# Gate and up projections of a float32 encoder layer with rows on partitions instead of hidden columns

## The chip, the core and the metric

The kernel runs on one core of a Trainium2 chip. A core has a matrix engine (TensorE, in the profile PE, with PEld for its weight loads), VectorE (DVE), ScalarE (ACT), GpSimd (POOL) and SyncE (SP); SP, ACT and POOL each issue DMAs from a queue of their own. Matmuls write to PSUM, eight banks of 128 partitions by 512 floats. Everything else lies in SBUF, 128 partitions wide, or outside in DRAM. The metric is the device time of one execution in microseconds (us), the median over runs.

## The reference

One encoder layer over 256 rows of 2048 features: a block of four mixers, a cross attention over 256 memory rows, and a SwiGLU feed-forward, each added to the residual, then a last normalisation. What the change touches is the last part:

```python
def swiglu(h, w_gate_up, w_down):
    gate, up = jnp.split(h @ w_gate_up, 2, axis=-1)
    return (jax.nn.silu(gate) * up) @ w_down
...
x = x + swiglu(rms_norm(x, norm_g[l, 2]), w_gate_up[l], w_down[l])
return rms_norm(x, final_norm_g)
```

`w_gate_up` is 2048 x 11264 (twice D_FF = 5632), `w_down` 5632 x 2048.

## The kernel before

Each float32 matrix product is made of reduced-precision (float32r) parts: an operand is split into a high part and the remainder (`split`, L202: ScalarE casts the high part, VectorE subtracts), and high x high, high x low and low x high are summed in PSUM. An activation tile, or slot, is 128 features by 512: 256 rows' high parts, then their low parts. Weights come as one stream, `Stream`: the host packs them in the order of use, 16 blocks of 128 x 128 to a 1 MB slab. SP loads slabs into three `raw` buffers. `_half` (L77) splits half a slab (8 blocks) into `wh` (cast on ScalarE, L104) and `wl` (subtraction on VectorE, L105), three buffers each. `take` (L109) hands out blocks, and makes halves so that two lie ahead of the one in use.

There are two ways to multiply. In `gemm`/`mm` (L294 to L341) a weight block is the stationary operand: one matmul of `wh` with all 512 columns of the slot (L301), one of `wl` with the 256 high ones (L302). The output has columns of the weight on partitions, and `merge` (L308) adds the two parts. In `gemm_rows` (L343) and in `prod` within `down` the slot is stationary and four weight blocks stream by: three matmuls of 512 columns for each half of the rows (L353 to L355, L785 to L787). The output has rows on partitions.

Work beside the matmuls is put in order by `Background`: generators that yield a delay. After each matmul step `poll` (L154) goes through those that are due, by the matmul time that has passed (`pe`) and the VectorE time still owed (`dve`, less than `OWED` = 0.9). `drain` runs one to its end. The instructions so traced get their final place on each engine from a scheduler; `keep_place` (L219) ties an instruction behind the one traced before it on its engine.

`mlp` (L724) runs after the attention, whose last product `w_xo` goes through `gemm`. Its input is `h3`, 16 slots, of which the last four are split by `rest` (L571) while the first matmuls run. Over 44 pairs of column tiles (gate, up) `gemm` makes 16 matmul pairs each; the first four tiles run over k = 0 to 11, then over 12 to 15. The evacuation `ev` merges, multiplies by the row factor `rs` (from `rstd_later`: sums of squares by L247, a factor for each row, spread over a bank by L278), takes the Silu on ScalarE (L735), multiplies by up, and splits the product into `f[j]`, the slot that down needs. So the 44 slots of `f` stand ready, features on partitions, with no turning.

`turn` (L751) brings the first 12 of 16 residual tiles to rows on partitions meanwhile: VectorE transposes 32 x 32 blocks within a tile (L758), four DMAs write the blocks to their places in `xrows` outside (L761), and six DMAs read rows back (L765). POOL issues these.

`down` (L772) multiplies `f` by `w_down`, with rows on partitions, in four quarters `c` of 512 output columns, k = 0 to 43 in each. After quarters 0 to 2 the residual is added and squares are summed. Quarter 3 begins by turning the residual's last four tiles on PE into its PSUM banks (eight matmuls, L818), so that the products are added to them. Its last 12 k are held back and run one half of the rows after the other, with the normalisation behind each. The last 32 blocks of the weights lie in `st.places`, here the slots of `h3`, free by then.

Of the kernel before, what the change touches and what calls it, by code (L numbers as in the profile page):

```python
# [13 lines left out]
F32 = mybir.dt.float32  # L14
# [21 lines left out]

HELD = 32

ROWS = ((256, 512), (768, 832), (NBLK - 16 * FT, NBLK))

LATE = 12

# [125 lines left out]
class Block:  # L168
# [171 lines left out]
        if last:  # L340
            group(n - 4, 4, last, before_last)  # L341

    def gemm_rows(self, w, col, slots, done=None):  # L343

        nc = self.nc
        ps = [self.gbank() for _ in range(2)]
        nk = len(slots)
        for k in range(nk):
            wh, wl = self.st.take(w, k, col, 4)
            for r in range(2):  # L350
                hi = slots[k][:, r * P:(r + 1) * P]
                lo = slots[k][:, R + r * P:R + (r + 1) * P]
                nc.tensor.matmul(ps[r][:, :], hi, wh, start=k == 0, stop=False)  # L353
                nc.tensor.matmul(ps[r][:, :], hi, wl, start=False, stop=False)  # L354
                nc.tensor.matmul(ps[r][:, :], lo, wh, start=False, stop=k == nk - 1)  # L355
            if done:
                done(k)
            self.bg.pe(1.407)
            self.bg.poll()
        return ps  # L360


    def run(self):
        nc, cp = self.nc, self.cp
        st = self.st
        self.act = [cp.tile([P, 512], F32R, name=f"act{i}") for i in range(24)]
        self.res = [cp.tile([P, 4, R], F32, name=f"res{i}") for i in range(4)]
        self.resk = lambda i: self.res[i // 4][:, i % 4, :]
        self.vec = cp.tile([P, NV], F32, name="vec")
        self.ones = cp.tile([P, P], F32, name="ones")  # L370
        self.ident = cp.tile([P, P], F32, name="ident")
        self.acc = cp.tile([P, R], F32, name="acc")
        self.mg = cp.tile([P, 16], F32, name="mg")
        self.eps = cp.tile([P, 8], F32, name="eps")[:, 0:1]
        self.gap(cp, 224)

        self.kd = nc.dram_tensor("keys", (P, 16 * R), F32, kind="Internal").ap()
        self.xr = nc.dram_tensor("xrows", (R, D), F32, kind="Internal").ap()
        self.vd = nc.dram_tensor("values", (P, 8 * 512), F32, kind="Internal").ap()
# [26 lines left out]
    def mixers(self):  # L406
# [76 lines left out]
        with tc.tile_pool(name="mid", bufs=1) as mid:  # L483
            gl = Gla(self, mid)
            with tc.tile_pool(name="hyp", bufs=1) as hyp, tc.tile_pool(name="k2", bufs=8) as k2:
                hy = Hyena(self, hyp, k2)

                mem0 = hy.piece()[:, 0:R + 16]
                nc.sync.dma_start(mem0, self.t["mem0"])
                self.bg.add(prepare(mid))  # L490

                def ev_k(i, p):
                    if i == 8:
                        for k in range(0, KT, 4):
                            self.load_x(k, 4)
                    nc.gpsimd.dma_start(self.kd[:, i * R:(i + 1) * R], self.merge(p))

                self.gemm("w_xkv", [i * P for i in range(16)], h, ev_k, first=(8, [[k] for k in range(KT)]), before=start_m)
                for hd in range(4):
                    for r, p in enumerate(self.gemm_rows("w_xkv", D + hd * 512, h, start_x if hd == 3 else None)):  # L500
# [12 lines left out]
                self.gemm("w_in", [256, 384, 0, 128], h, lambda i, p: gl.feed(i, self.merge(p)))  # L513
                for r, p in enumerate(self.gemm_rows("w_in", 512, h)):
# [209 lines left out]
    def mlp(self):  # L724
        tc, nc, act = self.tc, self.nc, self.act
        with tc.tile_pool(name="fp", bufs=1) as fp:
            self.gap(fp, 192)
            f = act[4:12] + [fp.tile([P, 512], F32R, name=f"f{i}") for i in range(36)]
            box = {}

            def ev(i, p):
                u = self.merge(p)
                self.tt(u, u, box["rs"], ALU.mult)
                if i % 2 == 0:
                    nc.scalar.activation(u, u, AF.Silu)  # L735
                    box["g"] = u
                else:
                    self.tt(u, u, box["g"], ALU.mult)
                    self.split(f[i // 2], u)

            cols = []
            for j in range(FT):
                cols += [j * P, DFF + j * P]
            ready = [self.late, self.bg.add(self.rstd_later(self.acc, D, box))]
            turned = self.bg.add(self.turn())
            self.gemm("w_gate_up", cols, self.h3, ev, first=(4, [list(range(12)), list(range(12, 16))]),
                      before=lambda n: n and [self.bg.drain(g) for g in ready])
            self.bg.drain(turned)
            self.down(f)

    def turn(self):  # L751

# [19 lines left out]
    def down(self, f):  # L772
# [2 lines left out]


        nc, st = self.nc, self.st
        h3 = self.h3
        st.places = [(h3[2 * i], h3[2 * i + 1]) for i in range(8)]
        ss = self.rp.tile([P, 24], F32, name="rc", tag="rc")  # L780

        def prod(p, r, k, wh, wl, start, stop):
            hi = f[k][:, r * P:(r + 1) * P]
            lo = f[k][:, R + r * P:R + (r + 1) * P]
            nc.tensor.matmul(p[:, :], hi, wh, start=start, stop=False)  # L785
            nc.tensor.matmul(p[:, :], hi, wl, start=False, stop=False)  # L786
            nc.tensor.matmul(p[:, :], lo, wh, start=False, stop=stop)  # L787
# [4 lines left out]
        def norm(p, r):  # L792
# [9 lines left out]
            for c in range(4):  # L802
# [6 lines left out]
                    nc.vector.tensor_scalar(out=x, in0=x, scalar1=a, scalar2=None, op0=ALU.mult)  # L809
                (nc.scalar if c == 1 else nc.sync).dma_start(self.t["out"][r * P:(r + 1) * P, c * 512:(c + 1) * 512], x)  # L810

        held = []
        for c in range(4):
            ps = [self.gbank() for _ in range(2)]
            if c == 3:
                for r in range(2):
                    for j in range(4):
                        nc.tensor.matmul(ps[r][:, j * P:(j + 1) * P], self.resk(12 + j)[:, r * P:(r + 1) * P], self.ident,  # L818
                                         is_transpose=True, start=j == 0, stop=False)
            for k in range(FT):  # L820
                wh, wl = st.take("w_down", k, c * 512, 4)
                if c == 3 and k >= FT - LATE:
                    held.append((k, wh, wl))
                    continue
                for r in range(2):
                    prod(ps[r], r, k, wh, wl, c < 3 and k == 0, c < 3 and k == FT - 1)
            if c < 3:
                for r in range(2):
                    x = self.half(c, r)
# [12 lines left out]
        nc.scalar.mul(fg[:, 3 * 512:4 * 512], fg[:, 3 * 512:4 * 512], 0.375)  # L842
        for r in range(2):
            for k, wh, wl in held:
                prod(ps[r], r, k, wh, wl, False, k == FT - 1)
            norm(ps[r], r)


# [540 lines left out]
```

## Time and profile before

| | us |
|---|---|
| median of 3 runs | 1506.02 |
| lowest, highest | 1505.64, 1507.26 |
| profiled execution | 1506.59 |
| its span, first to last instruction | 1504.8 |
| attention's last product ends, gate and up begin | about 762 |
| first matmul of down (L785) | 1250.4 |
| first turning matmul of the last quarter (L818) | 1435.2 |
| granted TensorE clock, mean | 0.999 of full speed |

How to read the profile: rows of the timeline give start, duration, engine, line, operation, out<-in and count, and in brackets the idle time before and what ended it. Rows of groups give line, engine, operation, out<-in, shape and count, then busy us and mean ns of one, then idle us before and what ended that. Matmuls are pipelined, and the duration of one overlaps the next, so their pace is the distance between starts. A row of waits or "idle before" counts only where the engine that waits is the one that others wait for.

### The profile page before, as it was taken

Reading aid. Unit: us, or ns where it says so; the run is one execution under the profiler, and the core shown is the slowest. Engines: PE = TensorE matmul, PEld = TensorE weight load, DVE = VectorE, ACT = ScalarE, POOL = GpSimd, SP = SyncE. Lnnn points to the kernel's source line nnn. Section 1 sums busy time; section 2 is a strip of 40 time slices with the busy share of each in tenths; the row PEclk is TensorE's granted clock in tenths of the full one; section 3 lists DMA queues with packets and bytes.
Section 4 is the critical chain, followed back from the end, with each engine's and each line's share of the span. In section 5 each row is a group of like instructions: output and inputs, shape, how many; then the busy total and the mean of one; then the engine's idle time right before and its main releaser. Section 6 shows DMA issues by size and latency. Waiting matters only on the chain.

```text
span 1504.8 us, 21369 instructions
## 1 busy us (share of the span) xinstructions
PE 1494.2 (99%) x8288; PEld 1288.5 (86%) x8288; DVE 997.8 (66%) x1551; ACT 784.7 (52%) x1236; POOL 68.6 (5%) x128
## 2 busy tenths in 40 slices
PE   9999999999999999999999999999999999999997
PEld 8887788889899888888888888888888888888886
DVE  6676768778776777877767666666666665444444
ACT  6565555547545556756555444444444444434344
POOL 0100100000000001100015100000000000000000
PEclk9999999999999999999999999999999999999999
DMA  9965554454446555544557655555555555555554
GB/s 355 347 245 202 187 197 160 151 193 143 177 155 216 193 196 203 191 149 170 194 179 248 211 181 190 195 196 182 185 193 196 191 182 186 196 188 179 193 193 142
DMA packets 51255, 294.68 MB, mean 196 GB/s; under 512 B 7086, under 2 KB 8399, under 8 KB 19537
## 3 DMA queue, kind: packets, MB, share of 16 engines
q1 hardware_dynamic: 45632, 281.11, 52.7%
q0 software_dynamic: 5088, 11.54, 2.3%
q8 instruction: 65, 1.06, 0.3%
q10 hardware_dynamic: 432, 0.66, 0.1%
q14 instruction: 38, 0.30, 0.1%
HBM read 285.42 MB, written 7.86 MB: 195 GB/s over the span
## 4 chain that ended last, share of the span: by engine, by line
PE 97%; ACT 1%; DVE 1%; DMA 0%; issue 0%; SPq 0%; ACTq 0%
PE pg L301 42%; PE pg L302 22%; PE pg L785 5%; PE pg L787 5%; PE pg L786 5%; PE pg L353 3%; PE pg L355 2%; PE pg L354 2%; PE pg L298 1%; PE pg L299 1%; PE pm L301 1%; PE pm L717 1%; PE pm L690 0%; PE pm L302 0%; DMA raw<-in_W 0%
## 5 line engine op out<-in xcount | busy, mean ns | idle before, releaser
L301 PE MATMUL pg<-act,wh 128*128 128x512 f32 x2704 | 945.9, 393 | 0.3 <-ACT wh L104 0.3
L105 DVE TENSOR_TENSOR wl<-raw,wh 128x1024 fp32r<-128x1024 f32 (+1 forms) x503 | 612.2, 1218 | 426.4 <-ACT wh L104 421.7
L104 ACT CAST wh<-raw 128x1024 fp32r<-128x1024 f32 (+1 forms) x503 | 524.7, 1044 | 589.0 <-PE pg L301 231.3
L302 PE MATMUL pg<-act,wl 128*128 128x256 f32 x2880 | 805.9, 280 | 0.2 <-DVE wl L105 0.2
L301 PEld LDWEIGHTS pg<-act,wh 128*128 128x128 f32 x2704 | 507.9, 188 | 112.7 <-ACT wh L104 0.6
L302 PEld LDWEIGHTS pg<-act,wl 128*128 128x128 f32 x2880 | 540.9, 188 | 2.3 <-issue 1.2
L785 PE MATMUL pg<-wh,f 128*128 128x512 f32 x272 | 107.9, 397 | 0.0
L787 PE MATMUL pg<-wh,f 128*128 128x512 f32 x272 | 107.8, 396 | 0.0
L786 PE MATMUL pg<-wl,f 128*128 128x512 f32 x272 | 107.6, 395 | 0.0
L196 DVE TENSOR_TENSOR tmp<-pg,tmp 128x256 f32<-128x256 f32 x174 | 72.6, 418 | 7.4 <-ACT tmp L308 6.1
L308 ACT COPY tmp<-pg 128x256 f32<-128x256 f32 x173 | 62.8, 364 | 11.4 <-PE pg L302 10.9
L353 PE MATMUL pg<-wh,act 128*128 128x512 f32 x160 | 64.0, 400 | 0.0
L355 PE MATMUL pg<-wh,act 128*128 128x512 f32 x160 | 63.0, 394 | 0.0
L354 PE MATMUL pg<-wl,act 128*128 128x512 f32 x160 | 62.9, 393 | 0.0
L787 PEld LDWEIGHTS pg<-wh,f 128*128 128x128 f32 x272 | 51.3, 189 | 12.0
L786 PEld LDWEIGHTS pg<-wl,f 128*128 128x128 f32 x272 | 51.3, 189 | 11.9
L785 PEld LDWEIGHTS pg<-wh,f 128*128 128x128 f32 x272 | 51.4, 189 | 11.8
L298 PE MATMUL pg<-act,wh 128*128 128x256 f32 x176 | 50.6, 288 | 0.0
L299 PE MATMUL pg<-act,wh 128*128 128x256 f32 x176 | 49.3, 280 | 0.0
L196 DVE TENSOR_TENSOR tmp<-tmp,rs 128x256 f32<-128x256 f32 x88 | 37.1, 423 | 2.7
L353 PEld LDWEIGHTS pg<-wh,act 128*128 128x128 f32 x160 | 30.1, 188 | 9.5 <-issue 1.7
L355 PEld LDWEIGHTS pg<-wh,act 128*128 128x128 f32 x160 | 30.1, 188 | 6.5
(263 smaller groups left out, 1222.8 us busy)
## 6 DMA issues: line engine op xcount, KB each, us to landing
raw<-in_W SPq DMA_DIRECT2D x246, 1024.0 KB, 4.8
raw<-in_W SPq DMA_DIRECT2D x11, 512.0 KB, 7.5
res<-in_xT SPq DMA_DIRECT2D x8, 512.0 KB, 5.8
k<-in_mem SPq DMA_DIRECT2D x8, 256.0 KB, 7.9
k<-in_x SPq DMA_DIRECT2D x8, 256.0 KB, 9.0
keys<-tmp POOLq DMA_DIRECT2D x16, 128.0 KB, 5.7
values<-tmp POOLq DMA_DIRECT2D x16, 128.0 KB, 2.1
mr<-keys POOLq DMA_DIRECT2D x16, 128.0 KB, 5.0
```

The source lines that it names most:

```text
L104: nc.scalar.copy(wh[:, a:b], r[:, a:b])
L105: nc.vector.tensor_tensor(out=wl[:, a:b], in0=r[:, a:b], in1=wh[:, a:b].bitcast(F32), op=ALU.subtract)
L196: self.nc.vector.tensor_tensor(out=out, in0=a, in1=b, op=op)
L298: self.nc.tensor.matmul(p[:, 0:R], wh, slot[:, 0:R], start=start, stop=False)
L301: self.nc.tensor.matmul(p[:, :], wh, slot[:, :], start=start, stop=False)
L302: self.nc.tensor.matmul(p[:, 0:R], wl, slot[:, 0:R], start=False, stop=stop)
L353: nc.tensor.matmul(ps[r][:, :], hi, wh, start=k == 0, stop=False)
L354: nc.tensor.matmul(ps[r][:, :], hi, wl, start=False, stop=False)
L355: nc.tensor.matmul(ps[r][:, :], lo, wh, start=False, stop=k == nk - 1)
L785: nc.tensor.matmul(p[:, :], hi, wh, start=start, stop=False)
L786: nc.tensor.matmul(p[:, :], hi, wl, start=False, stop=False)
L787: nc.tensor.matmul(p[:, :], lo, wh, start=False, stop=stop)
```

## The change

Gate and up now go through `gemm_rows`, which takes one or more column groups at once and works in parts. Eleven times a group of 512 gate columns and one of 512 up columns are made, rows on partitions (the first time both together, k = 0 to 11 and 12 to 15). The row factor is then one number per partition, an operand of the Silu and of the product. The product is turned back by VectorE's 32 x 32 transposes and eight DMAs to a DRAM tensor `hidden`; four DMAs read slots' worth of it back, and `fetch` splits them into `f`. The first 28 slots are fetched during gate and up, three reads ahead; the last 16 take the tiles of `h3` and are fetched during down, six ahead. The last weights' places become 16 tiles of their own. The turning of the residual's last quarter moves ahead of down's first quarter, into two `pm` banks that are kept. `ROWS`, which sets an offset of the weight buffers for rows-on-partitions stages, now covers gate and up.

```diff
-ROWS = ((256, 512), (768, 832), (NBLK - 16 * FT, NBLK))
+ROWS = ((256, 512), (768, 832), (NBLK - 48 * FT, NBLK))
...
+    def part_rows(self, p, r, slot, wh, wl, start, stop):
+
+        hi, lo = slot[:, r * P:(r + 1) * P], slot[:, R + r * P:R + (r + 1) * P]
+        self.nc.tensor.matmul(p[:, :], hi, wh, start=start, stop=False)
+        self.nc.tensor.matmul(p[:, :], hi, wl, start=False, stop=False)
+        self.nc.tensor.matmul(p[:, :], lo, wh, start=False, stop=stop)
+        self.bg.pe(0.687)
+
+    def gemm_rows(self, w, cols, slots, done=None, parts=None, before=None):
+
+
+        ps = [[self.gbank() for _ in range(2)] for _ in cols]
         nk = len(slots)
...
+        for part, ks in enumerate(parts or [range(nk)]):
+            if before:
+                before(part)
+            for k in ks:
+                for p, col in zip(ps, cols):
+                    wh, wl = self.st.take(w, k, col, 4)
+                    for r in range(2):
+                        self.part_rows(p[r], r, slots[k], wh, wl, k == 0, k == nk - 1)
+                if done:
+                    done(k)
+                self.bg.poll()
         return ps
...
+            f = act[4:12] + [fp.tile([P, 512], F32R, name=f"f{i}") for i in range(20)] + self.h3
+            with tc.tile_pool(name="gp", bufs=2) as gp:
+                self.gate_up(gp, f)
+            with tc.tile_pool(name="hp", bufs=1) as hp:
+                self.gap(hp, 64)
+                held = [hp.tile([P, 512], F32R, name=f"held{i}") for i in range(HELD // 2)]
+                self.st.places = list(zip(held[0::2], held[1::2]))
+                self.down(f)
+
+    def gate_up(self, gp, f):
+
+        nc = self.nc
+        box, g, stored = {}, {}, []
+
+        def norm():
+            box["col"] = self.rstd_begin([[self.acc]], D)
+            yield
+
+        def gate(ps):
+            for r in range(2):
+                g[r] = gp.tile([P, 512], F32, name=f"g{r}", tag=f"g{r}")
+                nc.scalar.activation(g[r], ps[r], AF.Silu, scale=box["col"][:, r:r + 1])
+
+        def up(j, ps):
+            for r in range(2):
+                h, u = (gp.tile([P, 512], F32, name=n, tag=n) for n in ("h", "u"))
+                self.stt(h, ps[r], box["col"][:, r:r + 1], g[r], ALU.mult, ALU.mult)
+                self.bg.dve(512)
+                nc.vector.transpose(u, h)
+                to = self.ff[j * 512:(j + 1) * 512, r * P:(r + 1) * P].rearrange("(b f) t -> f b t", f=32)
+                for a in range(4):
+                    nc.gpsimd.dma_start(to[:, :, 32 * a:32 * a + 32],
+                                        u[32 * a:32 * a + 32, :].rearrange("f (b t) -> f b t", t=32))
+            stored.append(j)
+
+        def fetch(k0, k1, ahead, pause):
+
+            m = {}
+            for k in range(k0, k1 + ahead):
+                if k < k1:
+                    while len(stored) <= k // 4:
+                        yield
+                    m[k] = self.tmp()
+                    nc.gpsimd.dma_start(m[k], self.ff[k * P:(k + 1) * P, :])
+                if k >= k0 + ahead:
+                    mark = len(nc.cur_bb.bb.instructions)
+                    self.split(f[k - ahead], m.pop(k - ahead))
+                    self.keep_place(mark)
+                    self.have = k - ahead + 1
+                    yield pause
+
+        ready = [self.late, self.bg.add(norm())]
+        turned = self.bg.add(self.turn())
+        ps = self.gemm_rows("w_gate_up", [0, DFF], self.h3, parts=[range(12), range(12, 16)],
+                            before=lambda n: n and [self.bg.drain(g) for g in ready])
+        gate(ps[0])
+        up(0, ps[1])
+        early = self.bg.add(fetch(0, FT - 16, 3, 2.0))
+        for j in range(1, DFF // 512):
+            gate(self.gemm_rows("w_gate_up", [j * 512], self.h3)[0])
+            up(j, self.gemm_rows("w_gate_up", [DFF + j * 512], self.h3)[0])
+        for x in (turned, early):
+            self.bg.drain(x)
+        self.bg.add(fetch(FT - 16, FT, 6, SOON))
...
+        end = [self.bank() for _ in range(2)]
+        for r in range(2):
+            for j in range(4):
+                nc.tensor.matmul(end[r][:, j * P:(j + 1) * P], self.resk(12 + j)[:, r * P:(r + 1) * P], self.ident,
+                                 is_transpose=True, start=j == 0, stop=False)
         held = []
         for c in range(4):
-            ps = [self.gbank() for _ in range(2)]
-            if c == 3:
...
+            ps = end if c == 3 else [self.gbank() for _ in range(2)]
             for k in range(FT):
...
                 for r in range(2):
-                    prod(ps[r], r, k, wh, wl, c < 3 and k == 0, c < 3 and k == FT - 1)
+                    self.part_rows(ps[r], r, f[k], wh, wl, c < 3 and k == 0, c < 3 and k == FT - 1)
+                self.bg.poll()
+                while self.have < min(FT, k + 3):
+                    self.bg.step(self.bg.q[0])
```

More of the change, by code (lines that the diff above doesn't have):

```diff
@@ L341, in gemm @@
             group(n - 4, 4, last, before_last)
-    def gemm_rows(self, w, col, slots, done=None):
-        nc = self.nc
-        ps = [self.gbank() for _ in range(2)]
-        nk = len(slots)
[L348 to L359, printed above, removed]
+    def part_rows(self, p, r, slot, wh, wl, start, stop):
[6 more added lines that the diff above has]
+        ps = [[self.gbank() for _ in range(2)] for _ in cols]
+        nk = len(slots)
+        for part, ks in enumerate(parts or [range(nk)]):
[9 more added lines that the diff above has]
+                self.bg.poll()
         return ps
@@ L378, in run @@
         self.xr = nc.dram_tensor("xrows", (R, D), F32, kind="Internal").ap()
+        self.ff = nc.dram_tensor("hidden", (DFF, R), F32, kind="Internal").ap()
         self.vd = nc.dram_tensor("values", (P, 8 * 512), F32, kind="Internal").ap()
@@ L499, in mixers @@
                 for hd in range(4):
-                    for r, p in enumerate(self.gemm_rows("w_xkv", D + hd * 512, h, start_x if hd == 3 else None)):
+                    for r, p in enumerate(self.gemm_rows("w_xkv", [D + hd * 512], h, start_x if hd == 3 else None)[0]):
                         for c in range(2):
@@ L513, in mixers @@
                 self.gemm("w_in", [256, 384, 0, 128], h, lambda i, p: gl.feed(i, self.merge(p)))
-                for r, p in enumerate(self.gemm_rows("w_in", 512, h)):
+                for r, p in enumerate(self.gemm_rows("w_in", [512], h)[0]):
                     nc.scalar.copy(gl.v[r], p)
@@ L727, in mlp @@
             self.gap(fp, 192)
[L728 to L749, printed above, removed]
+            f = act[4:12] + [fp.tile([P, 512], F32R, name=f"f{i}") for i in range(20)] + self.h3
@@ L777, in down @@
         nc, st = self.nc, self.st
-        h3 = self.h3
-        st.places = [(h3[2 * i], h3[2 * i + 1]) for i in range(8)]
         ss = self.rp.tile([P, 24], F32, name="rc", tag="rc")
[L782 to L787, printed above, removed]
         def squares(x, c, r):
@@ L810, in norm @@
                 (nc.scalar if c == 1 else nc.sync).dma_start(self.t["out"][r * P:(r + 1) * P, c * 512:(c + 1) * 512], x)
+        end = [self.bank() for _ in range(2)]
[3 more added lines that the diff above has]
+                                 is_transpose=True, start=j == 0, stop=False)
         held = []
         for c in range(4):
-            ps = [self.gbank() for _ in range(2)]
-            if c == 3:
[L816 to L819, printed above, removed]
+            ps = end if c == 3 else [self.gbank() for _ in range(2)]
             for k in range(FT):
@@ L844, in down @@
             for k, wh, wl in held:
-                prod(ps[r], r, k, wh, wl, False, k == FT - 1)
+                self.part_rows(ps[r], r, f[k], wh, wl, False, k == FT - 1)
             norm(ps[r], r)
```

## The prediction

> **What bounds the kernel now.** I read the page's engine table first, then the chain of waits, then TensorE's timeline.
>
> ```profile
> span 1504.8 us, 21369 instructions
> PE 1494.2 (99%) x8288; PEld 1288.5 (86%) x8288; DVE 997.8 (66%) x1551; ACT 784.7 (52%) x1236; POOL 68.6 (5%) x128
> PE 97%; ACT 1%; DVE 1%; DMA 0%; issue 0%; SPq 0%; ACTq 0%
> ```
>
> PE works for 99% of the span and makes up 97% of the chain that ended last. VectorE and ScalarE have a third and a half of their time free. So an edit is worth what it changes in PE's own pace, plus any wait it gives PE. The pace is read as start to start in the timeline, since each record of 0.28 to 0.40 us overlaps the next. First and last row of three stretches, gate and up, then down's first quarter, then its last:
>
> ```profile
> 899.79 0.28 PE L302 MATMUL pg<-act,wl 128*128 128x256 f32 x1
> ...
> 933.76 0.28 PE L302 MATMUL pg<-act,wl 128*128 128x256 f32 x1
> ...
> 1259.72 0.40 PE L786 MATMUL pg<-wl,act 128*128 128x512 f32 x1
> ...
> 1299.85 0.40 PE L787 MATMUL pg<-wh,f 128*128 128x512 f32 x1
> ...
> 1439.73 0.39 PE L786 MATMUL pg<-wl,act 128*128 128x512 f32 x1
> ...
> 1479.78 0.39 PE L787 MATMUL pg<-wh,f 128*128 128x512 f32 x1
> ```
>
> The first holds 98 pairs of L301 and L302: 33.97 us / 98 = 0.3466 us a pair. The second holds 172 steps in 40.13 us: 0.2333 us a matmul. The third holds 175 steps in 40.05 us: 0.2289 us. **One loop, with one shape, runs at two paces**, 1.9% apart. Between the second and third lie only the eight turning matmuls L818. I looked for the same switch elsewhere:
>
> ```profile
> 302.45 0.28 PE L302 MATMUL pg<-act,wl 128*128 128x256 f32 x1
> 302.57 0.40 PE L353 MATMUL pg<-wh,act 128*128 128x512 f32 x1
> ...
> 303.97 0.40 PE L353 MATMUL pg<-wh,act 128*128 128x512 f32 x1
> ...
> 100.12 0.40 PE L355 MATMUL pg<-wh,act 128*128 128x512 f32 x1
> ...
> 101.52 0.39 PE L355 MATMUL pg<-wh,act 128*128 128x512 f32 x1
> 101.75 0.39 PE L988 MATMUL pm<-w3h,hs 128*128 128x512 f32 x1
> ...
> 106.92 0.39 PE L353 MATMUL pg<-wh,act 128*128 128x512 f32 x1
> ...
> 111.27 0.39 PE L354 MATMUL pg<-wl,act 128*128 128x512 f32 x1
> ```
>
> Rows-on-partitions matmuls that follow the L301/L302 pairs directly are slow: 302.57 to 303.97 is 6 steps of 0.233, and 100.12 to 101.52 is too. After other matmuls have come between (L988 at 101.75), they are fast: 106.92 to 111.27 is 19 steps of 0.229. So the pace is not a property of tile or shape. It is kept from how the run of matmuls began.
>
> **The change part by part.**
>
> *Matmuls of gate and up.* Before: 88 column tiles x 16 = 1408 pairs, 1408 x 0.3466 = 488.0 us. After: 22 column groups of 512 (gate and up, 11 each) x 16 x 6 = 2112 matmuls of 512 columns; the columns streamed are the same. At the fast pace 2112 x 0.2289 = 483.4 us, **-4.6 us**; at the slow one 492.7 us, **+4.7 us**. Which holds depends on whether something breaks the run. The new stage starts behind `w_xo`'s pairs, so slow. Then `norm` issues `rstd_begin`, the only other matmuls of the stage:
>
> ```profile
> 767.09 0.34 PE pm L247 x4
> 772.88 0.66 PE pm L278 x2
> 1435.35 0.87 PE pg L818 x8
> ```
>
> These are rows of the chain. L247 now lies 5 us into the stage and stays, between the second and the latest the twelfth k of the first round, as the part boundary drains it. I take it as a breaker like L988 and L818; some 24 matmuls before it at the slow pace cost 24 x 0.0044 = 0.1 us. L278, which spread the row factor over a bank, falls away, since the factor is now one number per partition: **-0.7 us**.
>
> The Trainium skill ("TensorE: Matmul & The Clock Gate", Back-to-back issue gap) gives an isolated warm matmul N/2.4 + 2.5 ns, whatever ran before it. By it four blocks cost 1300 ns before and 1295 ns after, in all -1.8 us, and down would not change. The measured 1386 and 1373 ns lie over 5% above, and the two paces contradict it.
>
> *Down.* The eight L818 matmuls (0.87 us) move from ahead of the last quarter to ahead of the first, cost unchanged, 0. They need `res` rows 12 to 15, done before gate and up begin, and two `pm` banks, which nothing else needs then but the squares; two remain. They sit ahead of all of down, so its first three quarters, 3 x 44 x 6 = 792 matmuls, go at 0.2289 instead of 0.2333: **-3.5 us**. If they don't set the pace, 0.
>
> *Evacuation.* Nearest rows:
>
> ```profile
> L105 DVE TENSOR_TENSOR wl<-raw,wh 128x1024 fp32r<-128x1024 f32 x498 | 609.5, 1225 | 423.4 <-ACT wh L104 418.7 <-PE pg L302 2.1 <-ACT tmp L308 1.2
> L104 ACT CAST wh<-raw 128x1024 fp32r<-128x1024 f32 x498 | 522.3, 1049 | 586.0 <-PE pg L301 231.3 <-issue 153.5 <-PE pg L787 133.3
> L991 ACT ACTIVATE k<-k,vec 128x512 f32<-128x512 f32 x8 | 5.8, 724 | 0.1
> L196 DVE TENSOR_TENSOR k<-k,pm 128x512 f32<-128x512 f32 x10 | 6.8, 685 | 6.3 <-PE pm L989 6.3
> L196 DVE TENSOR_TENSOR f<-tmp,f 128x256 fp32r<-128x256 f32 x36 | 15.1, 419 | 0.0
> L204 ACT CAST f<-tmp 128x256 fp32r<-128x256 f32 x36 | 14.6, 404 | 0.0
> L200 DVE SCALAR_TENSOR_TENSOR act<-res,vec,act 128x256 fp32r<-128x256 f32 x32 | 15.1, 479 | 0.0
> L758 DVE STREAM_TRANSPOSE tmp<-res 128x256 f32<-128x256 f32 x12 | 5.2, 435 | 0.0
> ```
>
> 512 columns cost 685/419 = 1.63 times 256. Per group of 512 hidden columns ScalarE has two Silus (0.72) and four casts (0.40), 3.1 us; VectorE two products (1.63 x 0.479 = 0.78), two transposes (0.71) and four subtractions (0.42), 4.7 us. Before, VectorE had six operations of 0.42 for each of four tiles, 10 us. All lies beside 44 us of matmuls: 0. PE needs the banks again only after 16 x 6 x 0.229 = 22 us; in the first round gate's banks finish three to six matmuls ahead of up's, which covers most of their Silus. Price if not covered: two Silus, 1.4 us, once.
>
> *The way outside.* Each group issues eight writes of 64 KB and four reads of 128 KB on POOL's queue.
>
> ```profile
> L761 POOL DMA_DIRECT2D xrows<-tmp x48: 582/582/609, 765.0 to 834.0; - x48
> ...
> DMA to landing us min/median/max: 1.8/3.7/6.7
> ...
> q1 hardware_dynamic: 1979, 14.38, 53.5%
> q0 software_dynamic: 1856, 2.62, 12.5%
> res<-xrows POOLq DMA_DIRECT2D x6, 256.0 KB, 5.4
> ```
>
> The old `turn` has the same 128-byte runs. The two queue rows are the window 764 to 842 us that it fills: 12.5% for 2.62 MB against 53.5% for 14.38, so 1.28 times the time per byte. The new 88 x 64 KB out and 44 x 128 KB back, 11.5 MB, take 11.5/2.62 x 12.5% x 78 us = 43 us of all 16 engines over 484 us: 9% on top of 53%. Weights (SP's queue) stay ahead. On POOL, behind the writes stand reads and `turn`'s issues; down needs `turn` only after its first quarter.
>
> The danger is the hand-over. Let E be the end of up's last matmul. Products and transposes finish at E+1.5 and E+3.0; the eighth write leaves POOL at E + 1.5 + 8 x 0.58 = E+6.2 and lands at E+9.9; the read waits for all eight, then 0.6 + 5.4: E+15.9. In code order the planner lets the first split pass once 2.8 us of evacuation are worked off (E+5.5), and each further one 2.75 us later. Group 0's first split stands at E+5.5, that of groups 1 to 6 at E+13.8; the last sixteen begin at E+5.5 too, with older data, behind eight writes: E+12. ScalarE would block 10.4, 2.1 (six times) and 6.5 us, and behind it stand the weight casts L104, for which VectorE and PE wait. The cover is two halves of weights ahead, 5.5 us, less 1.05 + 1.23 to make the next: 3.2 us. So code order gives 7.2 + 0 + 3.3 = 10.5 us. The other end is 0:
>
> ```profile
> 762.24 0.36 ACT L308 COPY tmp<-pg 128x256 f32<-128x256 f32 x1
> 764.06 1.05 ACT L104 CAST wh<-raw 128x1024 fp32r<-128x1024 f32 x1 [1.47 <-PE pg L301]
> 765.02 0.41 ACT L234 ACTIVATE tmp<-res 128x256 f32<-128x256 f32 x1
> ```
>
> L234 squares the residual L308 evacuated, and comes in the code before the cast of a later half; on ScalarE the cast runs first. Instructions that are not ready are set behind ready ones, so I expect the casts ahead of splits that wait. I take 0.8 us, near that end.
>
> **Sum.** -4.6 + 0.1 - 0.7 + 0 - 3.5 + 0.8 = -7.9 us. The profiled execution took 1506.59 us (span 1504.8, 1.8 around it), 0.6 above the median of 1506.02, so the median becomes 1498.1; I say **1498**.
>
> **Rivals.**
>
> *Hand-over blocks (slower).* Casts stay behind splits, and writes and reads land 2 us later than the medians (6.7 is on record): 9.2 + 6 x 0.9 + 5.3 = 20 us, giving 1506 - 8.7 + 20 = 1517. It decides from 8.7 us of stalls on, about what the medians in code order make, so it starts as a draw. For: eleven hand-overs, one queue. Against: the order above.
>
> *L247 doesn't break the run.* Gate and up slow, down fast: +4.7 - 0.7 - 3.5 + 0.8 = +1.3, 1507.3. For: L247 has one column, unlike L988 and L818; no row shows it ahead of such matmuls.
>
> *No breaker works.* The change doesn't do what it seems to: +4.7 - 0.7 + 0.8 = +4.8, 1510.8. Against: two switches, L818 itself one.
>
> *The paces mix.* Each short wait of PE sets the run anew, either way. At the mean of 0.2311 gate and up cost 2112 x 0.2311 = 488.1, no gain, and down 1.7 less: -0.7 - 1.7 + 0.8 = -1.6, 1504.4. Against: neither pace was left within 40 us above. (The skill's formula would land there too, at 1504.2.)
>
> **Chances.** Forecast 0.66 (own range 1495 to 1503, small hand-over stalls included), hand-over 0.15, L247 0.10, no breaker 0.05, mixed paces 0.04. 0.2% is 3 us, about what a measurement of this kernel can tell. Below 1503: 0.68, with a little of the rivals; above 1509: 0.19; between: 0.13. The low end is the sum without stalls (1497.3) less 0.9 if the turns fill a bubble and 1.3 for spread and records: 1495. The high end takes in the L247 case and half a hand-over: 1509.
>
> **What would show it.** Steps of 0.229 in gate and up after L247, and in all of down; 0.233 in either refutes that term. L818 directly behind the last up matmul. ScalarE and VectorE without waits for the read of the hidden rows; PE idle, or casts waiting behind such a split, would show the hand-over. Turned out wrong: a span above 1502.

## The result and the profile after

The changed kernel took **1498.24 us** (median of 6 runs, 1497.69 to 1499.18), the kernel before in the same series 1506.49 (6 runs, 1505.64 to 1507.26): ratio 0.9946, 95% interval 0.9933 to 0.9959. The profiled execution took 1498.32 us with a span of 1496.5. The page, its engine table and the shares of the chain:

```profile
span 1496.5 us, 19811 instructions
PE 1485.9 (99%) x7582; PEld 1254.2 (84%) x7582; DVE 938.3 (63%) x1373; ACT 759.3 (51%) x1125; POOL 149.7 (10%) x260
PE 97%; ACT 1%; DVE 1%; DMA 0%; issue 0%; SPq 0%; ACTq 0%
```

TensorE still sets the end, with some 700 matmuls fewer, and POOL's busy time has more than doubled by the way outside. Where the 8.3 us of span came from is read from three starts on TensorE: gate and up's first matmul, down's first matmul, the end. First two rows of the timeline of the kernel before, then two of the kernel after:

```profile
761.15 0.39 PE L301 MATMUL pg<-act,wh 128*128 128x512 f32 x1
...
1250.38 0.40 PE L785 MATMUL pg<-wh,act 128*128 128x512 f32 x1
```

```profile
761.23 0.39 PE L346 MATMUL pg<-wh,act 128*128 128x512 f32 x1
...
1246.01 0.60 PE L857 MATMUL pm<-ident,res 128*128 128x128 f32 x4
1246.36 0.48 PE L346 MATMUL pg<-wh,act 128*128 128x512 f32 x1
```

Gate and up went from 1250.38 - 761.15 = 489.2 us to 1246.36 - 761.23 = 485.1 us: 4.1 less, although they now hold the eight turning matmuls. From there to the end it is 1504.8 - 1250.4 = 254.4 before and 1496.5 - 1246.4 = 250.1 after: 4.3 less, 0.9 of it the turning that left. The paces, from the first and last row of a stretch in gate and up and one in down's first quarter, kernel after:

```profile
899.69 0.39 PE L348 MATMUL pg<-wh,act 128*128 128x512 f32 x1
...
939.97 0.39 PE L347 MATMUL pg<-wl,act 128*128 128x512 f32 x1
...
1259.74 0.39 PE L347 MATMUL pg<-wl,f 128*128 128x512 f32 x1
...
1299.79 0.39 PE L348 MATMUL pg<-wh,act 128*128 128x512 f32 x1
```

Each of the two has the step of 0.2289 us (40.28 us / 176, 40.05 us / 175). Both terms on which the forecast rested are there. The other matmuls of gate and up, rows of the chain:

```profile
765.95 0.34 PE pm L247 x4
...
806.02 0.44 PE pm L857 x4
```

The row of L278 is gone. The turning matmuls (L857, the old L818) stand in two halves, one behind the first round of gate and up, one ahead of down: the scheduler took four of them 440 us early. 485.1 us less 2112 x 0.2289 = 483.4, L247 (0.3) and the turning (0.9) leaves 0.5 us for all waits of TensorE together.

How the hand-over went is read from ScalarE after the first round (timeline of the kernel after; in brackets the idle time before and what ended it):

```profile
805.66 1.26 ACT L757 ACTIVATE g<-pg,rc 128x512 f32<-128x512 f32 x2
806.82 1.05 ACT L104 CAST wh<-raw 128x1024 fp32r<-128x1024 f32 x1
809.48 1.05 ACT L104 CAST wh<-raw 128x1024 fp32r<-128x1024 f32 x1 [1.60 <-PE pg L348]
...
823.21 1.05 ACT L104 CAST wh<-raw 128x1024 fp32r<-128x1024 f32 x1 [1.70 <-PE pg L348]
824.16 0.40 ACT L204 CAST act<-tmp 128x256 fp32r<-128x256 f32 x1
```

Two Silus at the end of the round, then seven weight casts at 2.7 us apart, each waiting only for a free weight buffer, and then the first split, whose data had landed at 822.6. The split never stood in front of a cast. The table of waits over gate, up and down says the same of the whole stage (us in total, times, longest):

```profile
ACT wh L104 <- PE pg L348: 365.6, 228, 1.7
...
POOL tmp L779 <- DMA hidden<-u: 41.1, 8, 7.4
...
ACT f L204 <- DMA tmp<-hidden: 0.8, 1, 0.8
```

The reads wait on POOL for the writes to land, 41 us in all, which costs nothing there; ScalarE waits for a read once, 0.8 us. The transfers themselves, a row of the windows table for gate and up, before and after (the last two columns but one: granted clock and DMA share):

```profile
760.00:1246.00 486.00, 486.00 (x2805) 427.66 (x2804) 319.56 (x465) 236.73 (x353) 31.16 (x54) 1.00 0.56 195
```

```profile
760.00:1246.00 486.00, 486.00 (x2129) 398.43 (x2128) 257.44 (x276) 209.26 (x231) 104.27 (x173) 1.00 0.65 218
```

The share of the 16 DMA engines rose by 9 points, and TensorE is busy for the whole stretch in both.

### The profile page after: what moved, and what is told of

Read it like the earlier page. It is cut to its first block, busy times and chain, and to the rows that moved or that the text cites. A ratio compares the mean times of both kernels' runs of the same rounds, so it can differ in the third digit from the quotient of the medians.

```text
span 1496.5 us, 19811 instructions
## 1 busy us (share of the span) xinstructions
PE 1485.9 (99%) x7582; PEld 1254.2 (84%) x7582; DVE 938.3 (63%) x1373; ACT 759.3 (51%) x1125; POOL 149.7 (10%) x260
## 4 chain that ended last, share of the span: by engine, by line
PE 97%; ACT 1%; DVE 1%; DMA 0%; issue 0%; SPq 0%; ACTq 0%
PE pg L301 21%; PE pg L346 18%; PE pg L347 17%; PE pg L348 17%; PE pg L302 11%; PE pm L346 1%; PE pm L348 1%; PE pm L347 1%; PE pg L298 1%; PE pg L299 1%; PE pm L301 1%; PE pm L725 1%; PE pm L698 0%; PE pm L302 0%; DMA raw<-in_W 0%
## 5 line engine op out<-in xcount | busy, mean ns | idle before, releaser
L301 PE MATMUL pg<-act,wh 128*128 128x512 f32 x1296 | 457.7, 395 | 0.3 <-ACT wh L104 0.3
L302 PE MATMUL pg<-act,wl 128*128 128x256 f32 x1472 | 412.4, 280 | 0.2 <-DVE wl L105 0.2
L346 PE MATMUL pg<-wh,act 128*128 128x512 f32 x1008 | 397.1, 394 | 0.0
L347 PE MATMUL pg<-wl,act 128*128 128x512 f32 x1008 | 395.9, 393 | 0.0
L348 PE MATMUL pg<-wh,act 128*128 128x512 f32 x1008 | 392.9, 390 | 0.0
L301 PEld LDWEIGHTS pg<-act,wh 128*128 128x128 f32 x1296 | 243.6, 188 | 54.3 <-ACT wh L104 0.6
L302 PEld LDWEIGHTS pg<-act,wl 128*128 128x128 f32 x1472 | 276.8, 188 | 2.3 <-issue 1.2
L346 PEld LDWEIGHTS pg<-wh,act 128*128 128x128 f32 x1008 | 189.3, 188 | 45.8 <-issue 1.7
L348 PEld LDWEIGHTS pg<-wh,act 128*128 128x128 f32 x1008 | 189.3, 188 | 42.5
L347 PEld LDWEIGHTS pg<-wl,act 128*128 128x128 f32 x1008 | 189.5, 188 | 38.6
L346 PE MATMUL pg<-wh,f 128*128 128x512 f32 x120 | 47.3, 394 | 0.0
L348 PE MATMUL pg<-wh,f 128*128 128x512 f32 x120 | 47.0, 392 | 0.0
L347 PE MATMUL pg<-wl,f 128*128 128x512 f32 x120 | 46.6, 388 | 0.0
L308 ACT COPY tmp<-pg 128x256 f32<-128x256 f32 x85 | 30.9, 365 | 10.9 <-PE pg L302 10.8
L298 PEld LDWEIGHTS pg<-act,wh 128*128 128x128 f32 x176 | 33.2, 188 | 0.2
```

The source lines that it names most:

```text
L298: self.nc.tensor.matmul(p[:, 0:R], wh, slot[:, 0:R], start=start, stop=False)
L301: self.nc.tensor.matmul(p[:, :], wh, slot[:, :], start=start, stop=False)
L302: self.nc.tensor.matmul(p[:, 0:R], wl, slot[:, 0:R], start=False, stop=stop)
L308: self.nc.scalar.copy(t, p[:, R:512])
L346: self.nc.tensor.matmul(p[:, :], hi, wh, start=start, stop=False)
L347: self.nc.tensor.matmul(p[:, :], hi, wl, start=False, stop=False)
```

## The experiments

So the sum came out. But the timeline contradicts one of its reasons: gate and up followed the `w_xo` pairs directly, as down did before, and they were fast from the first matmul on, while L247 came only 4.7 us later. What sets the pace was therefore open, and so was whether the turning matmuls do anything. (Line numbers shift by a few lines where an edit adds some.)

**The turning alone, in the kernel before.**

```diff
+        end = [self.bank() for _ in range(2)]
...
+        for r in range(2):
+            for j in range(4):
+                nc.tensor.matmul(end[r][:, j * P:(j + 1) * P], self.resk(12 + j)[...], self.ident, is_transpose=True, ...)
...
         for c in range(4):
-            ps = [self.gbank() for _ in range(2)]
-            if c == 3:
...
+            ps = end if c == 3 else [self.gbank() for _ in range(2)]
```

> The kernel before, with the eight turning matmuls moved ahead of down's first quarter and nothing else. Prediction's theory (other matmuls in between set the run of rows-on-partitions matmuls to the fast pace): all of down steps at 0.2289 us instead of 0.2333 in the first three quarters, 792 x 0.0044 = 3.5 us off, median near 1503.0. Rival (the pace belongs to the quarter or its banks, not to what ran before): the first three quarters stay at 0.2333, time unchanged within 0.5 us.

1502.53 us (10 runs) against 1506.13: ratio 0.9975, interval 0.9965 to 0.9985. Timeline, down's first quarter:

```profile
1259.64 0.39 PE L785 MATMUL pg<-wh,act 128*128 128x512 f32 x1
...
1299.93 0.39 PE L787 MATMUL pg<-wh,f 128*128 128x512 f32 x1
```

176 steps in 40.29 us, 0.2289: with the turning matmuls between pairs and down, down is fast, and the 3.6 us are the predicted 3.5.

**The turning put back, in the kernel after.**

```diff
-        end = [self.bank() for _ in range(2)]
...
-            ps = end if c == 3 else [self.gbank() for _ in range(2)]
+            ps = [self.gbank() for _ in range(2)]
+            if c == 3:
+                for r in range(2):
+                    for j in range(4):
+                        nc.tensor.matmul(ps[r][:, j * P:(j + 1) * P], self.resk(12 + j)[...], self.ident, is_transpose=True, ...)
```

> The changed kernel, with the turning matmuls put back ahead of the last quarter. In the changed kernel gate and up are at 0.2289 us a step from their first matmul on. Theory A (a run keeps its pace): down takes the fast pace over from gate and up, and the time stays at 1498.2 within 0.7. Theory B (the prediction's sum, -3.5 us for the turning ahead): down's first three quarters go at 0.2333 and the time is 1501.7.

1498.36 us (4 runs), ratio to the kernel before 0.9948 (0.9933 to 0.9963): nothing lost against 1498.24. Down's first quarter:

```profile
1259.83 0.39 PE L348 MATMUL pg<-wh,f 128*128 128x512 f32 x1
...
1299.89 0.39 PE L346 MATMUL pg<-wh,act 128*128 128x512 f32 x1
```

175 steps in 40.06 us, still 0.2289. In the changed kernel the turning matmuls are not needed for the fast pace: down now follows matmuls of its own kind that are fast already.

**One or two more pairs ahead of down, in the kernel before.** If the kind of the last matmul set the pace, pairs like those before them would change nothing.

```diff
+        spare = self.bank()
+        for i in range(1):
+            nc.tensor.matmul(spare[:, :], h3[0][:, 0:P], h3[1][:, :], start=i == 0, stop=False)
+            nc.tensor.matmul(spare[:, 0:R], h3[2][:, 0:P], h3[3][:, 0:R], start=False, stop=i == 0)
...
```

> The kernel before, with one extra pair of matmuls of gate and up's own kind (512 and 256 columns, into a spare bank that nobody reads) between gate and up and down. Phase theory (entries from pairs whose last 512-column step was 0.228 us fell into the slow pace, the one after a 0.230 step did not, and these alternate): the extra pair shifts the alternation, down starts at 0.2289 us a step, 3.5 us less 0.35 for the pair. Kind theory (only matmuls of another kind break the slow run): down stays at 0.2333, time +0.35.

> As the one before with two extra pairs. Phase theory: the alternation is back where it was, down at 0.2333 us a step, time +0.7. If any insertion into another bank breaks the run: 0.2289, 3.5 us less 0.7. Kind theory: 0.2333.

One pair: 1502.45 us (one run). Two pairs: 1503.82 (one run; the span is 1502.0 against 1500.7). Down's first quarter with one pair, then with two:

```profile
1249.63 0.28 PE L816 MATMUL pm<-act,act 128*128 128x256 f32 x1
1249.75 0.39 PE L785 MATMUL pg<-wh,act 128*128 128x512 f32 x1
...
1259.83 0.39 PE L787 MATMUL pg<-wh,act 128*128 128x512 f32 x1
...
1299.88 0.39 PE L785 MATMUL pg<-wh,f 128*128 128x512 f32 x1
```

```profile
1259.36 0.39 PE L785 MATMUL pg<-wh,act 128*128 128x512 f32 x1
...
1299.87 0.39 PE L785 MATMUL pg<-wh,f 128*128 128x512 f32 x1
```

Both 0.2289 (175 steps in 40.05, 177 in 40.51). The theory of the kind falls with the first: down directly behind a pair, and fast. A theory of phase, by which two pairs should come out as none, missed the second. But the added pairs are not like the others, with operands elsewhere and another bank: their steps were 0.233 to 0.241 instead of 0.228 and 0.230. So a cleaner test was wanted, one that adds nothing strange.

**One pair or two left out, in the kernel before,** long before down.

```diff
         wh, wl = self.st.take(w, k, c)
+        if (w, c, k) in (("w_gate_up", 20 * P, 8),):
+            return
```

> The kernel before, with one pair of gate and up's matmuls left out in the middle of the stage (one k of one gate column tile is missing from the sum). Phase theory: the strict alternation of 0.230 and 0.228 us steps reaches down one place shifted, down is entered after a 0.230 step and starts at 0.2289 us, about 3.8 us off (3.5 and the pair). Rival (down entered straight from pairs is slow): 0.2333 us a step in its first three quarters, 0.3 us off.

> The kernel before, with two pairs of gate and up's matmuls left out in the middle of the stage (two k of one gate column tile). Phase theory: the alternation is in place again, down's first three quarters at 0.2333 us a step, 0.7 us off. If leaving a pair out breaks the run in another way, 0.2289 here too.

One left out: 1502.02 us (one run; the kernel before 1506.58 beside it). Two: 1505.64 (one run). Down's first quarter, one left out, then two:

```profile
1259.62 0.39 PE L787 MATMUL pg<-wh,act 128*128 128x512 f32 x1
...
1299.90 0.39 PE L789 MATMUL pg<-wh,f 128*128 128x512 f32 x1
```

```profile
1259.72 0.40 PE L789 MATMUL pg<-wh,act 128*128 128x512 f32 x1
...
1299.86 0.40 PE L787 MATMUL pg<-wh,f 128*128 128x512 f32 x1
```

0.2289 (176 steps in 40.28) and 0.2333 (172 steps in 40.14). The removed work is worth 0.35 or 0.7 us. With one pair left out 0.7 us more were there already at the first rows-on-partitions matmul of the program (98.24 against 98.95 us), long before the edit. The other 3.5 of the 4.6 us are the pace of down. It depends on whether one or two pairs are missing some 260 us earlier. That the number of pairs is odd or even fits both, though each is a single run. The trace's times in nanoseconds show what alternates: the step from L301 to L302 is 230 and 228 to 229 ns in turn.

```
kernel                          last L301->L302   first two steps   pace after
before (into down)                        228          236, 234       0.2333
after (into gate and up)                  230          228, 237       0.2289
before, one pair left out                 230          228, 236       0.2289
before, two pairs left out                229          236, 233       0.2333
after, one w_xo pair left out             229          236, 233       0.2333 at first
```

The step that follows a 230 is 228 and the run settles at the fast pace; the step that follows the other is 236 and the run stays slow. The ten traces with this layout (both kernels, the runs above and the next two) agree: all 23 entries from pairs straight into such a stage behind a 228 or 229 were slow, 20 of them into the same two early stages, and all 4 behind a 230 were fast. The last line is the next run.

**One `w_xo` pair left out, in the kernel after.**

```diff
+        if (w, c, k) in (("w_xo", 8 * P, 8),):
+            return
```

> The changed kernel, with one pair left out of the last attention product ahead of gate and up (one k of one column tile). Phase theory: gate and up are now entered after a 0.228 us step and begin at 0.2333 us; the first thing that breaks the even run (a wait of PE or the one-column matmuls L247, both within 5 us) sets 0.2289, so the time moves by less than 0.5 us. If neither breaks it, gate and up stay at 0.2333 and the time rises by up to 9 us.

1497.22 us (one run). The entry turned slow as it should, but not for long. Timeline:

```profile
760.11 0.40 PE L348 MATMUL pg<-wh,act 128*128 128x512 f32 x1
...
762.22 0.40 PE L348 MATMUL pg<-wh,act 128*128 128x512 f32 x1
...
762.94 0.50 PE L348 MATMUL pg<-wh,act 128*128 128x512 f32 x1
...
764.66 0.28 PE L247 MATMUL pm<-ones,acc 128*128 128x1 f32 x2
```

Nine steps in 2.11 us are slow (0.234). At 762.94 a weight load of TensorE had waited 0.3 us, and behind that the six steps up to L247 average 0.231. So in this run the slow entry mended itself, 1.7 us ahead of L247. (That the run is 1 us faster than the kernel after is not the stage: it began 1.1 us earlier, 0.35 of it the missing pair.) The kernel after has the same wait, for VectorE to free a bank:

```profile
764.05 0.19 PEld L346 LDWEIGHTS pg<-wh,act 128*128 128x128 f32 x1 [0.33 <-DVE tmp L196]
```

From the traces, in nanoseconds, the six steps between that wait and L247:

```
kernel                            steps                        mean
after                             235 233 235 230 231 234      233.0
after, turning put back           235 229 232 226 229 232      230.5
after, one w_xo pair left out     236 232 232 226 229 231      231.0
```

The kernel after had been fast, came out of the wait near the slow pace, and was fast again behind L247 (0.2289 from 766.47 to 805.86). With the turning put back, which changes nothing up to here, it came out fast. So a short wait can set the pace either way, and in the kernel after L247 stands where it turned fast. Six steps are few, and no run leaves L247 out: whether it breaks a run stays open.

**The hand-over in code order.** In the kernel after, each weight cast and subtraction of gate, up and down is tied behind the instruction that the code issues before it.

```diff
+        mark = len(self.nc.cur_bb.bb.instructions)
         edges = [0, 256, 512, 1024] if n == 0 else [0, 512, 1024] if n == 8 else [0, 1024]
...
+        if self.pin:
+            self.pin(mark)
...
+        self.st.pin = self.keep_place
```

> The changed kernel, with each weight cast and subtraction of gate, up and down tied behind the instruction traced before it on its engine, so that none is set ahead of a split that waits for its read. The prediction's working gives 10.5 us more (7.2 at the first hand-over, 0 at the next six, 3.3 at the last sixteen slots). With this chip's landings (first read 16.8 us after the last up matmul, the last sixteen's reads issued ahead of the writes) 16.8 - 5.5 - 3.2 = 8 us at the first hand-over and next to nothing later: 1506. Rival (the order is no matter, reads land in time): 1498, no wait of PE.

1506.21 us (one run; the kernel before 1506.58), span 1504.4, 7.9 more than the kernel after. ScalarE's timeline at the first hand-over, then TensorE's:

```profile
820.74 0.40 ACT L208 CAST act<-tmp 128x256 fp32r<-128x256 f32 x1 [10.76 <-DMA tmp<-hidden]
821.05 2.94 ACT L106 CAST wh<-raw 128x1024 fp32r<-128x1024 f32 x3
```

```profile
816.97 0.60 PE L862 MATMUL pm<-ident,res 128*128 128x128 f32 x4
822.15 1.22 PE L350 MATMUL pg<-wh,act 128*128 128x512 f32 x2 [4.58 <-ACT wh L106]
```

The split now stands behind two casts instead of seven, ScalarE waits 10.8 us for the read, three casts are late behind it, and TensorE stops for 4.6 us. That is not all of the 7.9. The windows around it (the last three columns are granted clock, DMA share and GB/s):

```profile
818.00:822.00 4.00, 0.00 (x0) 0.00 (x0) 0.42 (x1) 1.26 (x2) 3.50 (x7) 0.72 0.41 132
822.00:826.00 4.00, 3.81 (x8) 2.61 (x9) 3.50 (x3) 1.99 (x3) 4.00 (x8) 0.50 0.43 73
826.00:830.00 4.00, 4.00 (x17) 3.21 (x17) 1.23 (x1) 1.05 (x1) 3.34 (x6) 0.92 0.90 306
```

After the stop the granted clock is 0.50 from 819.8 to 826.6 us, and a matmul takes 0.427 instead of 0.229: 8 of them in 4 us instead of 17. The first ten steps after the stop take 4.67 us instead of 2.29, so TensorE loses another 2.4 us when it has work again. Two smaller stops, behind reads of later groups at 921 and 1098 us, cost 0.6 and 0.8 us. The expected 8 us came out, but only a little over half of them as the wait that was expected. The Trainium skill ("TensorE: Matmul & The Clock Gate", the part on the HAM clock gate) has an idle window of some 3.4 us halve the rate. This run agrees on the half rate, but it came sooner: the granted clock fell at 819.8 us, 2.2 us after TensorE's last work had ended at 817.6.

**The place of the weights.** The paces so far are those of one layout. `ROWS` gives rows-on-partitions stages another offset of the weight buffers, so the distance between the moving operand (the weights) and the stationary one (the slot) was varied. Taken modulo 256 bytes it is 64 in both kernels, but 0 for the last 32 blocks of the kernel before, which lie in slots. (Of the 24 matmuls on these in each half, the last 13 step at 0.2267, not 22 as the expectation below has it.) For the pairs, where the weights are the stationary operand, it is 160.

```diff
-        at = 0 if any(a <= n < b for a, b in ROWS) else 8
+        at = 48 if any(a <= n < b for a, b in ROWS) else 8
...
-                self.gap(hp, 64)
+                self.gap(hp, 256)
```

The gap moves the places of the last weights the same way. In the kernel after, 48 floats (192 bytes) on make the distance 0; 16 floats (64 bytes) on, with a gap of 128, make it 128; 48 in all stages, the pairs' too, is a third variant. The first edit alone, in the kernel before, is a fourth.

> The changed kernel, with the weight halves of the rows-on-partitions stages 48 floats (192 bytes) further on in their buffers and the held weights' places moved likewise, so that a streamed row starts a multiple of 256 bytes from the stationary slot instead of 64 bytes on. In the kernel before, the last 22 matmuls of each held half, whose weights lie a multiple of 256 bytes from the slot, step at 0.2267 us. Theory (the pace also follows the distance of the two operands): 0.2267 in all of gate, up and down, 2904 x 0.0022 = 6.4 us off, and near 1 us in the two earlier stages of this kind: 1491. Rival (0.2267 came from the quiet end, where casts, subtractions and loads have stopped): 0.2289 as before, 1498.

> As the one before, 16 floats (64 bytes) further on, a distance of 128 bytes. If the distance sets the pace, another pace than 0.2289 appears, better or worse, from the first matmul of this kind on; if it doesn't, 0.2289 and 1498.

> The changed kernel with the weight halves 192 bytes on in every stage, those with hidden columns on partitions too (there the distance of the two operands goes from 160 bytes to 0, modulo 256). Theory (distance 0 is best for any pair of operands): the pairs of 512 and 256 columns, now 0.3466 us, take 0.340 or less, some 1600 pairs, 10 us below 1490.5. Rival (a 256-column matmul has another best distance): the pairs slow down, and the time is above 1490.5.

> The kernel before with the weight halves of its rows-on-partitions stages 192 bytes on. Theory (pace by distance alone, no second pace at distance 0): its down and two earlier stages step at 0.2267 us: 792 x 0.0066 + 264 x 0.0022 + 480 x 0.0025 = 7.0 us off, 1499. Then the change is worth 1499 - 1490.5 = 8.5 us at this distance as well, now all of it in gate and up (488.0 against 2112 x 0.2267 = 478.8). Rival (a run entered straight from pairs is slow at any distance): down at 0.2333, 1505.

Kernel after, distance 0: **1490.52 us** (4 runs, 1489.84 to 1492.59) against 1506.02 before, ratio 0.9902 (0.9885 to 0.9918). Gate and up:

```profile
899.62 0.39 PE L348 MATMUL pg<-wh,act 128*128 128x512 f32 x1
...
939.96 0.39 PE L346 MATMUL pg<-wh,act 128*128 128x512 f32 x1
```

178 steps in 40.34 us: 0.2266, a third pace. Kernel after, distance 128: 1510.92 us (one run), the same stretch and down's:

```profile
899.76 0.40 PE L346 MATMUL pg<-wh,act 128*128 128x512 f32 x1
...
939.97 0.39 PE L348 MATMUL pg<-wh,act 128*128 128x512 f32 x1
...
1259.73 0.39 PE L348 MATMUL pg<-wh,act 128*128 128x512 f32 x1
...
1299.86 0.39 PE L346 MATMUL pg<-wh,act 128*128 128x512 f32 x1
```

0.2324 (173 steps in 40.21) and 0.2333 (172 in 40.13): the changed kernel at this distance is about 5 us slower than the kernel before at 64. The kernel before at 128 was not run. Kernel before, distance 0: 1499.36 us (4 runs), ratio 0.9956 (0.9941 to 0.9970), and down is at 0.2266 from the first quarter on, directly behind the pairs (178 steps in 40.34):

```profile
1259.62 0.39 PE L785 MATMUL pg<-wh,f 128*128 128x512 f32 x1
...
1299.96 0.39 PE L786 MATMUL pg<-wl,f 128*128 128x512 f32 x1
```

All weights moved: 1494.85 us (4 runs), ratio 0.9929 (0.9913 to 0.9946), so slower than with the rows-on-partitions stages alone. The spans of the two profiled executions differ by 3.3 us (1491.4 - 1488.1), and gate and up begin 3.4 us later (763.02 against 759.62), so all of it is lost before them. It is lost on the pairs, at distance 0 now. A run of them with all weights moved:

```profile
564.82 0.40 PE L301 MATMUL pg<-act,wh 128*128 128x512 f32 x1
...
589.90 0.40 PE L301 MATMUL pg<-act,wh 128*128 128x512 f32 x1
```

71 pairs in 25.08 us are 0.3532 us a pair; at distance 160 the same run has 0.3467. Other runs of pairs have 0.3467 at distance 0 too, the last 222 ahead of gate and up among them. So the pairs have two paces at distance 0, as the matmuls of 512 columns have at 64. Over the pairs before 700 us, some 1150, the mean is 0.3497 against 0.3468, 3.3 us. The best version that ran is the changed kernel with distance 0 in the rows-on-partitions stages.

## Why the prediction was right, and where not

**Gate and up, -4.6 + 0.1 - 0.7:** right in size: the stage lost 4.1 us with 0.9 of turning moved into it, so 5.0 without. The step "the new stage starts behind `w_xo`'s pairs, so slow" failed. It started fast, with the last pair in the other phase, and that was luck, since nothing in the prediction chose the phase; with one pair left out it did start slow, and a short wait ended that within 3 us. Whether L247 is "a breaker" stays open. In the kernel after the short wait ahead of it took the fast pace away, and the pace was fast again behind L247, as the term supposed; in two other runs it was fast already. So the two rivals with a slow gate and up failed too, but not for the reason given against them: their slow entry did not come, and where it was made to come it did not last.

**Down, -3.5:** the size is right (254.4 - 250.1 - 0.9 = 3.4), the reason only half. The turning matmuls do bring down to the fast pace where it follows pairs in the slow phase: the kernel before gained 3.6 us by them. In the changed kernel they bring nothing, as they could be put back without loss; there the gain comes from the stage before being of the same kind, and fast. "L818 directly behind the last up matmul" was half seen, since four of the eight had gone ahead.

**"The pace is not a property of tile or shape; it is kept from how the run of matmuls began":** right at this distance of the operands, and too narrow. With the distance 0 there was no slow pace behind the pairs, and one faster than both. With 128 nearly all was slow. The rival of mixed paces had one thing right: a short wait can set the run anew, either way. But from L247 on gate and up kept the fast pace.

**The hand-over, 0.8 of a possible 10.5:** right, and for the reason given. The casts ran ahead of the waiting splits, and TensorE lost 0.5 us in all. Tied to code order it cost 7.9 us, which would have eaten the gain (1506.21 against 1506.58), so the slower rival was a real one and decided by the order alone. Its working was off in its parts: TensorE's first stop was 4.6 us and not 7.2, the 2.4 us lost behind it at the half clock were in no term, two later hand-overs, put at 0, cost 0.6 and 0.8, and the 3.3 us at the last sixteen slots did not come, since their reads left ahead of the last group's writes.

**Evacuation and the way outside, 0:** right. ScalarE and VectorE kept their waits for free buffers, and the DMA share rose by the 9 points.

What the change is worth by itself depends on the layout: 8.3 us at distance 64, where some 3.4 are down's pace, and 1499.36 - 1490.52 = 8.8 at distance 0, where down's pace is the same in both. There gate and up took 489.2 us in the kernel before (759.48 to 1248.71) and 480.6 in the kernel after (759.62 to 1240.21), 0.9 of turning included, so the gain lies in them.

## What to carry to other kernels

Where TensorE is busy for 99% of the span, read the step between starts of equal matmuls in several stages: two paces for one shape are a lead worth 1 to 3% of a stage, and moving an operand buffer is the cheapest trial (here 192 bytes gained and 64 bytes lost). Try it stage by stage, since one place for all was worse here than one place per kind of stage. Where work outside returns through an engine that also prepares the weights, look in the trace for what stands ahead of the waiting instruction: the order there was worth 7.9 us.

## What was not expected of the hardware

A float32r matmul of 512 columns with its weight load had three paces: 0.2266 us with operands 0 bytes apart modulo 256, 0.2289 or 0.2333 at 64 bytes, 0.2324 to 0.2333 at 128. Other distances were not run for it. A pair of 512 and 256 columns had two as well, 0.347 or 0.353 us at distance 0, and 0.347 at 160. The cause behind the numbers is not shown. At 64 bytes the pace of 792 matmuls, down's first three quarters, went with a difference of 1 to 2 ns in the step ahead of them. A stop of TensorE of 4.6 us cost another 2.4 us, about 2 of it by the granted clock, which was 0.50 for 6.8 us, the last 4.5 of them with work.
